# Cross-attention keys moved from after the first block into its woven steps

## Chip, core and metric

The kernel runs on one core of one Trainium2 chip. The metric is device time in microseconds (us) of one execution. All work is in fp32 precision, made of two fp32r parts (a high part and the remainder), so that a product of matrices is three matmuls: high by high, high by low, low by high.

## What is computed

Two transformer blocks run one after the other over 1024 tokens of width 1024. The first has a sliding-window attention and a gated convolution side by side, an output projection and a feed-forward layer. The second has three attentions side by side, then a cross attention to a memory of 256 rows, then a feed-forward layer. Only the cross attention's keys and values, which need the memory and no token, are touched by the change:

```python
def _cross(h, m, w_cq, w_ckv, w_co):
    q = (h @ w_cq).reshape(b, s, CROSS_HEADS, CROSS_DIM)
    k, v = jnp.split(m @ w_ckv, 2, axis=-1)
    ...
x = x + _cross(_rmsnorm(x, norm_cross[l]), _rmsnorm(mem, norm_mem[l]), ...)
```

## The kernel before, in words

Every activation is held transposed, in tiles of 128 features by 512 tokens (a half `h` of 0 or 1), each with a high and a low part. Weights stream from one packed tensor, 128x512 at a time (a slot of four 128x128 blocks): `Weights.block` (line 124) loads a slot on SP's queue, ScalarE (ACT) casts the high part, and the low part is made in one of two ways. While `W.adding` is set (line 778 to line 1583, the whole first attention and convolution), ACT writes the negated copy and a DMA issued by GpSimd (POOL) adds to it (line 143); afterwards VectorE (DVE) subtracts (line 145). There are 3 buffers for raw slots and 8 for each part, and loads keep their order.

The first block's work is woven by hand. `weave_all` (line 231) walks over main steps, which are matrix products yielding after each tile, and after each yield it runs as many side jobs from one ordered list as the step's rate has paid for. `SEQ` names the main steps: `k` keys and values, `a b c d` the queries of four head pairs, `G H` two convolution inputs, `o` the output projection over the first two of eight feature tiles (16 tiles of six matmuls: 8 output rows for half 0, then 8 for half 1), `P` the convolution's pointwise product and its part of the output projection for half 1. `SRATES` holds a rate for each. The side jobs are 17 attention steps (`swa`, piped by one), two convolutions (`convolve`, 47 vector multiply-adds each), `first_cat`, which fetches the first attention outputs back through DRAM, and the layer norm of the convolution for half 1 and half 0 (`normed`). Whether `"x"` is in `SEQ` decides where the memory is normed (`cross_norm`, line 1017) and where its keys are computed (`cross_keys`, line 1040): with it, the norm is a job of no cost at place `XNJ` of the list and the keys are a main step; without it, `cross_norm` is called behind the last woven product (after line 1109), and `cross_keys` behind the second half's output projection, just ahead of `cross_values`:

```python
    gemm(out1, 2, cat, ..., group=8, k0=2, x0=2, halves=(1, 0))
    if not mem_normed:
        mem_normed.append(cross_norm())
    x = load_x()
    ...
    add_post(x, mixed, rmix, "mix_post", 1)
    sums.first(x.cut(1))
    run(out1b(0, rmix))
    ...
    if "x" not in SEQ:
        run(cross_keys())
    if "X" not in SEQ:
        run(cross_values())
```

`load_x` (line 1121) reads the residual again; `add_post` (line 1123) adds the normed first half of the block to it; `sums.first` prepares the operands of the feed-forward layer, of whose products (`p`, seven for each tile) the first group is called `p5` and needs the sums `s1`.

Tiles with the tag `v` (128x512 fp32) are drawn from a common stock of `BUFS["v"]` buffers. The normed input `hn` takes 32 of them until the last queries (`d`) are done and the bias table `t5` takes 4; `cross_norm` asks for 4 tiles for the memory and 8 for its normed parts, and the normed parts live until keys and values are done. `cross_norm` takes its PSUM tile from the tag `mm` (7 buffers), which also holds every projection's output and the tiles `mu` and `bc` of the layer norms, and its scratch from `tmp` (3 buffers), which `add_post` uses next. Which instruction is issued when on each engine is fixed before the run by a list scheduler, from the program's order and the buffers, and isn't adapted to the chip.

Of the kernel before, what the change touches and what calls it, by code (L numbers as in the profile page):

```python
# [36 lines left out]
MERGE = 0  # L37
MLAPER = 1.8
FOXPER = 1.1
BUFS = {'phi': 6, 'plo': 6, 'hi': 2, 'lo': 3, 'fs': 2, 'v': 36, 'u': 8, 'p': 4, 'g': 4, 'mm': 7, 's': 3, 't': 3, 'o': 2, 'tmp': 3, 'evt': 3, 'stg': 2, 'rbc': 3, 'turn': 2, 'pt': 2, 'small': 20, 'csmall': 8, 'wraw': 3, 'whi': 8, 'wlo': 8, 'x': 58, 'y': 16, 'ge': 12, 'wt': 5, 'wq': 7, 'r': 16, 'sum': 4, 'rsum': 3, 'f': 6, 'l': 3}  # L40
NPRE = (4, 2)
TAIL = 2
BYPOOL = (0, 0)
# [24 lines left out]
STARTP = 200  # L68
XNJ = 8
GATES = (1, 2)  # L70
SEQ = "kabGHcdoP"
SRATES = (0.0, 0.0, 0.0, 0.75, 0.75, 1.0, 1.0, 2.0, 1.5)
SWACOST = 1.0
PLUS = ()
CONV2 = 3
# [20 lines left out]
class Weights:  # L96
# [27 lines left out]
    def block(self, mat, k, c0, w=P):  # L124
# [6 lines left out]
        if off == 0:  # L131
            s = pos // 4
            raw = self.pool.tile([P, 512], F32, tag="wraw", name=f"wraw{s}", bufs=BUFS["wraw"])
            self.load(raw, s)
            hi = self.pool.tile([P, 512], F32R, tag="whi", name=f"whi{s}", bufs=BUFS["whi"])
            lo = self.pool.tile([P, 512], F32R, tag="wlo", name=f"wlo{s}", bufs=BUFS["wlo"])
            if s in FIRSTW:
# [14 lines left out]
    def quarter(self, mat, k, c0, n=4, step=1):  # L152
# [3 lines left out]
        s = len(self.order) // 4  # L156
        raw = self.pool.tile([P, 512], F32, tag="wq", name=f"wraw{s}", bufs=BUFS["wq"])[:, :n * P]
        self.load(raw, s, n * P)
# [3 lines left out]
    def parted(self, raw, eng=None):  # L162
        self.made += 1
        w = raw.shape[-1]
        hi = self.pool.tile([P, 512], F32R, tag="phi", name=f"xhi{self.made}", bufs=BUFS["phi"])[:, :w]
        lo = self.pool.tile([P, 512], F32R, tag="plo", name=f"xlo{self.made}", bufs=BUFS["plo"])[:, :w]
        self.nc.scalar.copy(hi, raw)  # L167
# [63 lines left out]
def weave_all(mains, jobs):  # L231

    due = 0.0
    jobs = list(jobs)
    ended = 0
    for main, per, *need in mains:
        while need and need[0] in jobs:
            due -= jobs[0].cost  # L240
            jobs.pop(0)()
        for w in main:
            due += per * w
            while jobs and due >= jobs[0].cost and jobs[0].after <= ended:
                due -= jobs[0].cost
                jobs.pop(0)()
        ended += 1
    for j in jobs:
        assert j.after <= ended
        j()  # L250


def job(f, cost=1.0, after=0):
    f.cost, f.after = cost, after
    return f
# [26 lines left out]
def run(main):  # L282
    for _ in main:
        pass
# [3 lines left out]
def encoder_decoder_kernel(ctx: ExitStack, tc: tile.TileContext, a: dict, order_out: list):  # L288
# [728 lines left out]
    def cross_norm():  # L1017
        mem = [vt("mem") for _ in range(4)]
        ms = [mem[i // 2][:, (i % 2) * 256:(i % 2) * 256 + 256] for i in range(8)]
        with tc.issue_after(W.last.ins):  # L1020
            for i in range(8):
                nc.sync.dma_start(ms[i], a["memT"][tsl(i), :])
        both = {}

        class Mem:
            def hi(self, k, h):
                if k not in both:
                    both[k] = vt("memn", F32R)
                return both[k][:, 0:256]

            def lo(self, k, h):
                return both[k][:, 256:512]

        mn = Mem()
        norm_apply(ms, mn, 0, "norm_mem", rstd(sumsq(ms), D, psum=mmps))
        return mn
# [3 lines left out]
    def cross_keys():  # L1040
        mn = mem_normed[0]
        for i in range(4):
            if i % 2 == 0:
                xk_ = vt("xk")
            bl = [W.block("xk", k, i * P) for k in range(8)]
            ps = mmps("xk")
            mm3(ps[:, :256], [(bl[k], (mn.hi(k, 0), mn.lo(k, 0))) for k in range(8)])
            with tc.high_priority(offset=EVP):
                copy(xk_[:, (i % 2) * 256:(i % 2) * 256 + 256], ps[:, :256])
            if i % 2:  # L1050
                nc.sync.dma_start(zx[i // 2], xk_)
            yield 0.5

    def cross_values():
        def ev_xv(t, ps):
            u = vt("xv")
            copy(u, ps)
            nc.sync.dma_start(zx[2 + t], u)

        yield from vgemm_steps("xv", 8, mem_normed[0], 2, ev_xv)  # L1060
# [20 lines left out]
    def pos(key):  # L1081
        return SEQ.index(key) + 1

# [10 lines left out]
    norm_job = job(lambda: mem_normed.append(cross_norm()), 0.0)  # L1094
    if "x" in SEQ:
        jobs.insert(XNJ, norm_job)
# [3 lines left out]
    for i in range(4):  # L1100
        mains["abcd"[i]] = lambda i=i: queries(i)
    ln_job = [j for j in jobs if getattr(j, "half", None) == 1][0]
    early = int("P" in SEQ)
    needs = {"P": (ln_job,), "o": (cat_job,), "x": (norm_job,)}
    weave_all([(mains[key](), SRATES[n]) + needs.get(key, ())
               for n, key in enumerate(SEQ)], jobs)

# [477 lines left out]
    for pr, names in zip(pre, AHEADW):  # L1585
        for name in names:
            pr.get(name)
# [4 lines that stand above are left out]
# [675 lines left out]
```

## Time and profile before

| | us |
|---|---|
| median of three runs (2411.0 to 2414.62) | 2414.3 |
| the profiled execution, its own time | 2412.51 |
| its span in the trace | 2410.7 |
| TensorE (PE) busy | 2347.0 (97%) |
| VectorE (DVE) busy | 1752.9 (73%) |
| ScalarE (ACT) busy | 1139.9 (47%) |
| GpSimd (POOL) busy | 267.2 (11%) |

The busy times are of the one profiled execution. A matmul counts as busy until its modelled end, so two that overlap in the pipe are counted once; what a matmul costs is read from the distance between starts. In the rows, an arrow in square brackets gives the time for which an engine had been idle before an instruction, and what ended the wait.

### The profile page before, as it was taken

The numbers are of one execution on the slowest core, as the hardware profiler recorded it, in microseconds if no ns is written. First come the engines' busy times: TensorE is split into PE (matmuls) and PEld (weight loads), VectorE is DVE, ScalarE is ACT, GpSimd is POOL, SyncE is SP. The second block draws the span as 40 slices with busy tenths as digits, with TensorE's granted clock in tenths as the row PEclk, the third lists the DMA queues.
The fourth block names the chain that finished last, engine by engine and source line by source line (L and its number), as shares of the span: only waits on it lengthen the run. The fifth ranks groups of instructions, "written<-read, shape, count | busy, mean of one in ns | idle before, by whom it ended". The sixth has DMA issues, their size and how long they took to land.

```text
span 2410.7 us, 34720 instructions
## 1 busy us (share of the span) xinstructions
PE 2347.0 (97%) x11892; PEld 1894.6 (79%) x11892; DVE 1752.9 (73%) x3391; ACT 1139.9 (47%) x2313; POOL 267.2 (11%) x343
## 2 busy tenths in 40 slices
PE   9999799999999999999999999998999999999998
PEld 7877587687788887878887778887888888877886
DVE  7999659997777656688545576787797777666667
ACT  6355555545555543234444353545554555452222
POOL 2110121012111100000001110000011111110000
PEclk9999899999999999999999999999999999999999
DMA  7532278359867799724644465123237768699952
GB/s 206 121 82 58 49 155 296 115 146 280 228 173 215 200 373 366 253 78 152 186 119 147 142 201 181 40 58 101 79 103 199 208 173 219 178 276 379 353 173 77
DMA packets 235025, 430.09 MB, mean 178 GB/s; under 512 B 26112, under 2 KB 38752, under 8 KB 234848
## 3 DMA queue, kind: packets, MB, share of 16 engines
q1 hardware_dynamic: 197872, 350.71, 42.9%
q0 software_dynamic: 36688, 76.97, 16.1%
q8 instruction: 94, 1.54, 0.3%
q14 instruction: 83, 0.68, 0.1%
q10 hardware_dynamic: 288, 0.18, 0.0%
HBM read 246.10 MB, written 126.62 MB: 155 GB/s over the span
## 4 chain that ended last, share of the span: by engine, by line
PE 81%; DVE 9%; DMA 6%; issue 2%; ACT 1%; POOL 0%; SPq 0%; DVEq 0%; POOLq 0%; ACTq 0%
PE p L538 9%; PE p L540 9%; PE p L539 9%; PE mm L539 8%; PE mm L538 8%; PE mm L540 8%; PE low L540 5%; PE low L538 5%; PE low L539 5%; PE tp L589 2%; PE lo L1920 1%; DMA ff<-zff 1%; DMA wraw<-wstream 1%; PE fo L603 1%; DVE conv L839 1%
## 5 line engine op out<-in xcount | busy, mean ns | idle before, releaser
L538 PE MATMUL p<-s,xhi 128*128 128x512 f32 x704 | 276.6, 394 | 0.6 <-ACT xhi L167 0.5
L539 PE MATMUL p<-s,xhi 128*128 128x512 f32 x704 | 277.0, 393 | 0.0
L540 PE MATMUL p<-s,xlo 128*128 128x512 f32 x704 | 271.6, 394 | 1.3 <-DVE xlo L168 1.3
L538 PE MATMUL low<-ff,xhi 128*128 128x512 f32 (+1 forms) x628 | 246.7, 393 | 4.2 <-ACT xhi L167 4.2
L540 PE MATMUL low<-ff,xlo 128*128 128x512 f32 (+1 forms) x628 | 244.8, 393 | 2.8 <-DVE xlo L168 2.8
L539 PE MATMUL low<-ff,xhi 128*128 128x512 f32 (+1 forms) x628 | 246.5, 392 | 0.0
L167 ACT CAST xhi<-wt 128x512 fp32r<-128x512 f32 (+1 forms) x248 | 148.7, 607 | 180.7 <-DVE wt L178 90.2
L538 PE MATMUL p<-x,xhi 128*128 128x512 f32 x528 | 209.0, 396 | 3.3 <-ACT lo L1307 1.7
L540 PE MATMUL p<-x,xlo 128*128 128x512 f32 x528 | 206.4, 395 | 1.9 <-DVE xlo L168 1.9
L539 PE MATMUL p<-x,xhi 128*128 128x512 f32 x528 | 207.7, 393 | 0.0
L168 DVE TENSOR_TENSOR xlo<-wt,xhi 128x512 fp32r<-128x512 f32 (+1 forms) x248 | 166.1, 673 | 52.2 <-ACT xhi L167 38.6
L168 DVE TENSOR_TENSOR xlo<-wraw,xhi 128x512 fp32r<-128x512 f32 (+1 forms) x228 | 150.5, 665 | 45.2 <-DMA lo<-s 10.7
L167 ACT CAST xhi<-wraw 128x512 fp32r<-128x512 f32 (+1 forms) x228 | 134.0, 599 | 97.3 <-PE low L539 60.3
L540 PEld LDWEIGHTS p<-s,xlo 128*128 128x128 f32 x704 | 132.2, 188 | 32.7 <-DVE xlo L168 2.5
L538 PEld LDWEIGHTS p<-s,xhi 128*128 128x128 f32 x704 | 132.2, 188 | 32.7 <-ACT xhi L167 2.1
L539 PEld LDWEIGHTS p<-s,xhi 128*128 128x128 f32 x704 | 132.2, 188 | 30.6
L538 PEld LDWEIGHTS low<-ff,xhi 128*128 128x128 f32 x628 | 119.1, 190 | 32.2 <-ACT xhi L167 5.3
L540 PEld LDWEIGHTS low<-ff,xlo 128*128 128x128 f32 x628 | 119.1, 190 | 30.6 <-DVE xlo L168 3.9
L539 PEld LDWEIGHTS low<-ff,xhi 128*128 128x128 f32 x628 | 119.0, 190 | 26.8
L1308 POOL DMA_DIRECT2D lo<-u x82 | 71.5, 881 | 540.2 <-ACT lo L1307 358.3
L140 ACT CAST whi<-wraw 128x512 fp32r<-128x512 f32 x143 | 86.7, 616 | 87.5 <-DMA wraw<-wstream 56.4
L538 PEld LDWEIGHTS p<-x,xhi 128*128 128x128 f32 x528 | 99.1, 188 | 29.0 <-ACT xhi L167 3.0
(433 smaller groups left out, 5576.1 us busy)
## 6 DMA issues: line engine op xcount, KB each, us to landing
wraw<-wstream SPq DMA_DIRECT2D x408, 256.0 KB, 3.4
ff<-zff SPq DMA_DIRECT2D x308, 256.0 KB, 5.3
zff<-hi SPq DMA_DIRECT2D x154, 256.0 KB, 4.5
zff<-lo SPq DMA_DIRECT2D x154, 256.0 KB, 4.3
lo<-u POOLq DMA_DIRECT2D x82, 256.0 KB, 5.0
lo<-s POOLq DMA_DIRECT2D x66, 256.0 KB, 6.1
wlo<-wraw POOLq DMA_DIRECT2D x56, 256.0 KB, 3.9
res<-zres SPq DMA_DIRECT2D x48, 256.0 KB, 5.9
```

What stands on the lines that cost most here:

```text
L140: nc.scalar.copy(hi, raw)
L167: self.nc.scalar.copy(hi, raw)
L168: ins = (eng or self.nc.vector).tensor_tensor(lo, raw, hi.bitcast(F32), op=ALU.subtract)
L538: nc.tensor.matmul(ps, lhsT=ah, rhs=bh, start=first and i == 0, stop=False, skip_group_check=shared)
L539: nc.tensor.matmul(ps, lhsT=ah, rhs=bl, start=False, stop=False, skip_group_check=shared)
L540: nc.tensor.matmul(ps, lhsT=al, rhs=bh, start=False, stop=last and i == n - 1, skip_group_check=shared)
L589: nc.tensor.transpose(ps[:, tsl(j)], pr[:, c0 + (g + j) * P:][:, :P], ident)
L603: nc.tensor.matmul(o[j * 64:j * 64 + 64, :P], lhsT=value(g + t, j), rhs=pts[j][t], start=g + t == 0, stop=g + t == nt - 1)
L839: nc.vector.scalar_tensor_tensor(d, s_, col, d, ALU.mult, ALU.add)
L1308: nc.gpsimd.dma_start(lo, t, accum_op=ALU.add)
L1920: nc.tensor.matmul(o[:, tsl(j)], lhsT=lv[t][:, h * P:h * P + P], rhs=pt[t], start=t == 0, stop=t == i)
```

## The change

The letter `x` enters `SEQ` between `d` (the last queries) and `o` (the output projection), with a rate of 1.0, and the stock of `v` buffers grows from 36 to 38. By the two conditions quoted above, `cross_norm` becomes a side job that the planner reaches at the end of step `c`, `cross_keys` runs between `d` and `o`, and both calls later on fall away. `cross_values` stays. As the keys now run while `W.adding` is set, the low parts of their eight weight slots are made by ACT and a POOL DMA.

```diff
-BUFS = {..., 'v': 36, ...}
+BUFS = {..., 'v': 38, ...}
...
-SEQ = "kabGHcdoP"
-SRATES = (0.0, 0.0, 0.0, 0.75, 0.75, 1.0, 1.0, 2.0, 1.5)
+SEQ = "kabGHcdxoP"
+SRATES = (0.0, 0.0, 0.0, 0.75, 0.75, 1.0, 1.0, 1.0, 2.0, 1.5)
```

## Rows read from the trace of the kernel before

**Rows 1.** The page, busy time by engine: the tensor engine.

```profile
PE 2347.0 (97%) x11892; PEld 1894.6 (79%) x11892; DVE 1752.9 (73%) x3391; ACT 1139.9 (47%) x2313; POOL 267.2 (11%) x343
```

**Rows 2.** Busy time by stretch: stretch, its length, then each engine's busy time.

```profile
core 0: us, PE busy (x) PEld busy (x) DVE busy (x) ACT busy (x) POOL busy (x), PEclk, DMA share, GB/s
160.00:200.00 40.00, 40.00 (x234) 30.65 (x233) 37.15 (x96) 20.68 (x58) 5.51 (x8) 1.00 0.40 91
200.00:240.00 40.00, 37.37 (x268) 28.82 (x268) 40.00 (x128) 24.58 (x79) 2.77 (x4) 0.91 0.11 33
240.00:268.00 28.00, 14.53 (x99) 9.11 (x98) 23.24 (x53) 13.83 (x44) 3.03 (x5) 0.79 0.00 0
268.00:300.00 32.00, 29.86 (x141) 22.68 (x141) 17.00 (x32) 20.84 (x39) 8.20 (x9) 0.87 0.43 90
300.00:350.00 50.00, 50.00 (x239) 40.37 (x238) 29.55 (x51) 27.69 (x52) 11.67 (x14) 1.00 0.69 152
350.00:384.00 34.00, 34.00 (x156) 27.75 (x154) 24.31 (x48) 16.36 (x32) 8.04 (x10) 1.00 0.90 278
384.00:480.00 96.00, 86.33 (x440) 68.89 (x439) 94.53 (x157) 58.04 (x103) 6.87 (x5) 0.96 0.52 173
480.00:520.00 40.00, 39.87 (x179) 32.04 (x179) 39.89 (x67) 16.92 (x31) 1.48 (x2) 1.00 0.39 108
```

**Rows 3.** Timeline of PE, 260 to 270: start, length, line, tiles, idle before.

```profile
260.56 2.08 PE L995 MATMUL mu<-lns,constr 128*128 128x512 f32 x2 [5.99 <-DVE lns L987]
267.43 1.02 PE L498 MATMUL bc<-constr,sum 128*64 128x1 f32 x16 [4.79 <-DVE sum L455]
268.96 0.63 PE L539 MATMUL mm<-cat,whi 128*128 128x512 f32 x1
269.39 0.63 PE L540 MATMUL mm<-cat,wlo 128*128 128x512 f32 x1
```

**Rows 4.** Timeline of ACT and DVE: the output projection's tiles leave PSUM.

```profile
216.25 1.04 ACT L965 COPY mixed<-mm 128x512 f32<-128x512 f32 x2
...
271.34 0.69 DVE L963 COPY mixed<-mm 128x512 f32<-128x512 f32 x1 [2.69 <-PE mm L540]
```

**Rows 5.** DVE groups by shape, 300 to 380: the memory's norm (busy, mean ns).

```profile
L519 DVE SCALAR_TENSOR_TENSOR y<-mem,const,bc 128x256 f32<-128x256 f32 x8 | 3.6, 476 | 0.2 <-PE bc L507 0.2
L427 DVE TENSOR_TENSOR memn<-y,memn 128x256 fp32r<-128x256 f32 x8 | 3.3, 420 | 1.5 <-ACT memn L426 1.4
L452 DVE TENSOR_TENSOR sum<-sum,sq 128x256 f32<-128x256 f32 x6 | 2.3, 424 | 1.2 <-ACT sq L450 1.2
```

**Rows 6.** Tile view of `xk`: keys' matmuls and copies (ns min/median/max).

```profile
L540 PE MATMUL xk<-memn,wlo x32: 276/282/579, 384.2 to 407.5; 128*128 128x256 f32 x32
L422 DVE COPY xk<-xk x2: 411/414/416, 397.2 to 411.0; 128x256 f32<-128x256 f32 x2
```

**Rows 7.** Timelines of PE and DVE: distances between starts in the keys.

```profile
384.10 0.28 PE L539 MATMUL xk<-memn,whi 128*128 128x256 f32 x1
384.22 0.28 PE L540 MATMUL xk<-memn,wlo 128*128 128x256 f32 x1
...
386.70 1.28 DVE L145 TENSOR_TENSOR wlo<-wraw,whi 128x512 fp32r<-128x512 f32 x2
```

**Rows 8.** The page, DMA issues: the low parts made by accumulating DMAs.

```profile
wlo<-wraw POOLq DMA_DIRECT2D x56, 256.0 KB, 3.9
```

**Rows 9.** Timelines of PE, DVE, SP, 354 to 380: around the first residual add.

```profile
354.82 0.69 DVE L427 TENSOR_TENSOR cat<-mm,cat 128x512 fp32r<-128x512 f32 x1 [4.49 <-ACT cat L426]
...
357.07 0.60 PE L507 MATMUL bc<-const 128*128 128x128 f32 x4
...
365.60 11.92 SPq L703 DMA_DIRECT2D x<-xT  x13
...
366.15 0.47 DVE L519 SCALAR_TENSOR_TENSOR y<-mem,const,bc 128x256 f32<-128x256 f32 x1
367.48 0.74 DVE L1128 SCALAR_TENSOR_TENSOR pn<-mixed,const,bc 128x512 f32<-128x512 f32 x1
379.90 0.69 DVE L1130 TENSOR_TENSOR x<-x,pn 128x512 f32<-128x512 f32 x1 [1.43 <-DMA x<-xT]
```

**Rows 10.** Timelines of DVE and PE: the first feed-forward products.

```profile
402.90 0.40 PE L538 MATMUL p<-s,xhi 128*128 128x512 f32 x1
403.10 0.68 DVE L427 TENSOR_TENSOR s<-s,s 128x512 fp32r<-128x512 f32 x1
403.14 0.39 PE L539 MATMUL p<-s,xhi 128*128 128x512 f32 x1
```

More of the change, by code (lines that the diff above doesn't have):

```diff
@@ L39 @@
 FOXPER = 1.1
-BUFS = {'phi': 6, 'plo': 6, 'hi': 2, 'lo': 3, 'fs': 2, 'v': 36, 'u': 8, 'p': 4, 'g': 4, 'mm': 7, 's': 3, 't': 3, 'o': 2, 'tmp': 3, 'evt': 3, 'stg': 2, 'rbc': 3, 'turn': 2, 'pt': 2, 'small': 20, 'csmall': 8, 'wraw': 3, 'whi': 8, 'wlo': 8, 'x': 58, 'y': 16, 'ge': 12, 'wt': 5, 'wq': 7, 'r': 16, 'sum': 4, 'rsum': 3, 'f': 6, 'l': 3}
+BUFS = {'phi': 6, 'plo': 6, 'hi': 2, 'lo': 3, 'fs': 2, 'v': 38, 'u': 8, 'p': 4, 'g': 4, 'mm': 7, 's': 3, 't': 3, 'o': 2, 'tmp': 3, 'evt': 3, 'stg': 2, 'rbc': 3, 'turn': 2, 'pt': 2, 'small': 20, 'csmall': 8, 'wraw': 3, 'whi': 8, 'wlo': 8, 'x': 58, 'y': 16, 'ge': 12, 'wt': 5, 'wq': 7, 'r': 16, 'sum': 4, 'rsum': 3, 'f': 6, 'l': 3}
 NPRE = (4, 2)
```

## The prediction

> **What bounds the kernel now.** The page comes first: PE is busy 97% of the span [rows 1], so a change that leaves PE's work alone can gain only where PE waits. Busy time by stretch shows where that is near the keys [rows 2]. From 200 to 268 us PE is busy 51.9 of 68 us while DVE has no idle time up to 240: the first block's attention and convolutions keep DVE full, and PE waits for them. PE's timeline shows how that ends: 5.99 us of waiting for DVE's sums of the last convolution, then 4.79 us for the layer norm's squares [rows 3]. From 300 to 384 PE has no idle time and DVE has plenty. From 384 to 480, where the keys are now, PE lacks 9.7 us and DVE only 1.5: the residual add, the operand sums and the weight splits of the feed-forward layer are DVE's, and PE waits again. From 480 on PE is full. So there are two stages bounded by DVE with one bounded by PE between them, and the change moves work from the second to the first. What counts is what it moves on DVE.
>
> **The change, part by part.**
>
> *The keys on PE.* Four tiles of eight blocks and three matmuls are 96 matmuls of 256 columns. The tile view lists 32 for each of three lines [rows 6]; starts are 0.12 us apart where none waits [rows 7], so 11.5 us of PE work move. At the new place PE has 16.1 us without work (200 to 268, [rows 2]), so they fit and cost nothing there by themselves. If that cover is gone, the price is those 11.5 us.
>
> *The memory's norm on DVE.* It has 8 multiplies, 8 subtractions, 6 additions and a last addition: 3.6 + 3.3 + 2.3 us busy [rows 5] and 0.4 (one more addition at 424 ns), 9.6 us; with DVE's two copies of keys (0.41 us each, [rows 6]) 10.4. Back to back, DVE starts every 0.60 us an instruction that lasts 0.68 (two in 1.28, [rows 7]), so by that ratio 9.2 us. The job stands ahead of the last convolution in the list, so it goes ahead of the layer norm that PE waits for. It can use DVE's idle time ahead of 200, 2.9 us in 160 to 200 [rows 2], and I take half. The layer norm's sums come 9.2 - 1.5 = **7.7 us later** (bounds 0, if DVE's gaps took all of it, and 9.2).
>
> *Order on PE behind the layer norm.* Six of the output projection's sixteen tiles have left PSUM by 217; the seventh is multiplied only behind `bc` and leaves at 271.34 [rows 4]. That is where the list puts the layer norm: with rate 2.0 and two attention jobs ahead of it, it falls between the sixth and seventh tiles, and the later tiles, of the same tag `mm`, keep behind its `mu` and `bc`. With the change the two attention jobs are paid for by `x` (four yields of 0.5 at rate 1.0), so the layer norm falls behind the second tile. Four tiles that now run while PE would wait move behind it: 4 x 6 matmuls x 0.23 us between starts (402.90 to 403.14 is 0.24, [rows 10]) = **5.5 us later** (bounds 0, if the scheduler orders them otherwise, and 5.5).
>
> *The norm's few matmuls* leave the stage bounded by PE: a third of a `bc` group and two transposes (four take 0.60 us, [rows 9]), **-0.6**.
>
> *The low parts of the keys' weights.* DVE no longer makes them: 8 at a distance of 0.60 us [rows 7], 4.8, and with the two copies at 0.36 (0.41 by the same ratio) 5.5 us off the second stage. At the new place ACT makes 8 negated copies more and POOL issues 8 accumulating DMAs, each landing in 3.9 us [rows 8]. ACT is busy 38.4 of 68 us there and POOL 5.8 [rows 2]; I cost them at nothing. What is queued behind them: POOL's widening copies of the attention's reciprocals and SP's round trip of `first_cat`; PE waits for DVE longer than for either.
>
> *What the old place of the norm held up.* The norm of the mixed half is ready when its `bc` is transposed, at 357.07. But `add_post` starts at 367.48, behind the last scratch tile of the memory's norm (366.15), and the residual's loads start at 365.60, so that the first add waits for them until 379.90 [rows 9]. With the norm gone the scratch is free, and the loads need only `v` buffers, of which two are new. DVE idles 9.7 us between 350 and 384 [rows 2], and the norm's two passes there, 6.9 us busy [rows 5], about 6.1 at the ratio above, fall away: 15.8 us. Of these 4.49 [rows 9] and some 2 us of the norm lie ahead of the transposes and can't take the add. The other 9 can take most of `add_post` (16 instructions, 9.6 us at 0.60). So `s1`, whose last part now ends at 403.78 [rows 10], and what follows come 9 + 5.5 = **14.5 us earlier** against the stretch ahead. Bounds: 5.5, if the loads come no earlier; above, what PE leaves: its 9.7 us of waiting [rows 2] and the 11.5 us of the keys, 21.
>
> The sum against the profiled execution's own time of 2412.5 us (span 2410.7 and 1.8 around it; the median of the runs is 1.8 higher): 7.7 + 5.5 - 0.6 - 14.5 = -1.9. Against the median, 2414.3 - 1.9 = **2412.4 us**.
>
> *A rule weighed.* In 240 to 268 the granted clock is 0.79 on average, and right behind the waits matmuls start 0.43 us apart instead of 0.23 [rows 2, 3], which is the 1.2 GHz level after PE had idled. The Trainium skill ("TensorE: Matmul & The Clock Gate", Part 1) says that the throttled state is the default and activity releases it. By that rule the keys in these gaps would keep the clock up and give back up to ten such starts, 2 us, and the sum would be -4; by the rows alone PE still idles as long just ahead of `bc`, and the sum stays.
>
> **The rivals.**
>
> *The keys fill the gap, and the order gives* (faster). If the scheduler puts output tiles into PE's waits ahead of the layer norm, the 5.5 us don't arise, and tiles now behind `bc` (13.8 us of PE work in ten tiles) come ahead; what remains of the 7.7 is what the layer norm itself holds up, about 4. 4 - 0.6 - 14.5 = -11: 2403. For it: PE has 16 us there. Against it: the scheduler had that chance before and left 10.8 us of waiting next to tiles that were ready [rows 3, 4].
>
> *The residual's loads don't come earlier* (slower). SP's queue is in order, and the loads stand behind weight loads that wait for buffers. If the first is still issued some 20 us or less ahead of its first use's old time, the second stage gives back only the 5.5 us of DVE work and a little idle time, 7: 7.7 + 5.5 - 0.6 - 7 = +5.6, 2420. It decides from the point where the first load is issued less than 3 us earlier than now, measured from the end of the half's projection (350).
>
> *The keys don't get there* (slower still; the change doesn't do what it says). The memory and its normed parts need 12 `v` buffers, and 36 of 38 are taken until the last queries are done. If the normed memory comes so late that the keys fall behind the layer norm, their 11.5 us stand in the stage bounded by PE: 13.2 + 11.5 - 0.6 - 14.5 = +9.6, 2424. Against it: the queries end near 200, 60 us ahead of the layer norm.
>
> **How the numbers follow.** The forecast's case has 0.42, with a range of its own of 2405 to 2419 (halves of the two uncertain terms); the faster rival 0.28, the loads 0.22, the late keys 0.08. About 0.2%, 4.8 us, is what a measurement can tell from no change. Faster: 0.26 of the faster rival and 0.12 of the forecast's case. Slower: 0.13 of the loads, 0.07 of the late keys, 0.04 of the forecast's case. Same: the remaining 0.38. Eight times in ten the time should lie between 2399, which takes in the faster rival with a few us of clock, and 2422; both signs hold much of the chance.
>
> **What would show it.** Right, step by step: keys' matmuls between 200 and 250; `bc` of the first layer norm some 8 us later than 267.4, with two output tiles ahead of it and fourteen behind; the pointwise product some 13 us later; the first residual add directly behind the transposes of `bc`; `s1` some 14 us earlier against the end of the half's projection; PE full again from about 480. Wrong would be a `bc` no later than now (DVE had room), more than two output tiles ahead of it, or a first add still waiting for the residual's load. What would overturn the sum altogether is a later stage that moves: two more `v` buffers can change the order there too, and no row of before can price that.

## The result, and the profile after

| | before | after |
|---|---|---|
| median of four runs each, side by side (us) | 2413.0 (2411.0 to 2414.6) | 2425.4 (2424.0 to 2426.9) |
| profiled execution: span (us) | 2410.7 | 2425.1 |
| TensorE (PE) busy (us) | 2347.0 | 2356.2 |

The ratio is 1.0054, with a 95% interval of 1.0042 to 1.0066: the change makes the kernel slower by about 13 us. The forecast was 2412.4, with 2422 as its upper end.

The stretches of [rows 2] in the kernel after:

```profile
160.00:200.00 40.00, 37.87 (x222) 28.75 (x222) 37.99 (x108) 21.38 (x66) 3.97 (x6) 0.87 0.30 73
200.00:240.00 40.00, 37.10 (x237) 30.52 (x237) 38.14 (x103) 20.78 (x63) 6.27 (x9) 0.87 0.19 47
240.00:268.00 28.00, 22.38 (x132) 17.00 (x132) 20.24 (x47) 15.22 (x39) 7.42 (x10) 0.77 0.79 179
268.00:300.00 32.00, 28.38 (x160) 22.07 (x158) 20.34 (x54) 20.89 (x54) 2.70 (x3) 0.83 0.05 17
300.00:350.00 50.00, 45.37 (x212) 35.89 (x211) 23.27 (x40) 25.60 (x51) 11.38 (x14) 0.93 0.66 169
350.00:384.00 34.00, 31.16 (x141) 24.69 (x140) 16.12 (x26) 15.96 (x29) 9.14 (x11) 0.95 0.76 173
384.00:480.00 96.00, 90.83 (x400) 72.19 (x399) 84.24 (x136) 51.78 (x92) 7.18 (x9) 0.98 0.58 184
480.00:520.00 40.00, 32.82 (x141) 24.36 (x142) 36.52 (x62) 16.22 (x28) 7.24 (x2) 0.83 0.13 41
```

PE is busier between 240 and 268 (22.4 us against 14.5), as meant. But DVE, the engine that bounds this part, is *less* busy there (20.2 against 23.2), and PE now idles where it had no idle time at all: from 300 to 384, and from 480 to 520.

Where the time went is read best from a few instructions that both traces have, as the time from each to the next. "Last add" is the last addition that gathers the output projection of half 1, then of half 0; "gate" is the 577th `p` matmul with a low weight part in the first feed-forward layer; "cross" the first scores (`xs`) of the second block's cross attention; "gate 2" the 625th such `p` matmul, in the second block's feed-forward layer.

| us | start to layer norm's `bc` | to half 1's last add | to half 0's last add | to gate | to cross | to gate 2 | to the end |
|---|---|---|---|---|---|---|---|
| before | 267.4 | 81.9 | 42.2 | 444.2 | 796.4 | 117.2 | 661.2 |
| after | 284.8 | 93.6 | 38.4 | 444.5 | 793.6 | 110.5 | 659.7 |
| difference | +17.4 | +11.7 | -3.8 | +0.3 | -2.8 | -6.7 | -1.5 |

The differences make the +14.4 us of the spans. The first block loses 25.5 us up to the gate; 11 come back much later, in code that the change doesn't touch.

The rows that answer to [rows 3, 6, 9, 10], of the kernel after, from PE's timeline (start, length, line, tiles, idle before):

```profile
225.49 0.38 PE L538 MATMUL xk<-memn,whi 128*128 128x256 f32 x1
...
277.80 1.03 PE L995 MATMUL mu<-lns,constr 128*128 128x512 f32 x2
...
284.78 0.63 PE L498 MATMUL bc<-constr,sum 128*64 128x1 f32 x16 [3.62 <-DVE sum L455]
...
384.75 0.60 PE L507 MATMUL bc<-const 128*128 128x128 f32 x4
...
415.81 0.39 PE L538 MATMUL p<-s,xhi 128*128 128x512 f32 x1
```

and from SP's and DVE's:

```profile
333.30 2.58 SPq L703 DMA_DIRECT2D x<-xT  x5
```

```profile
385.39 2.06 DVE L1128 SCALAR_TENSOR_TENSOR pn<-mixed,const,bc 128x512 f32<-128x512 f32 x3 [1.78 <-PE bc L507]
387.98 1.89 DVE L1130 TENSOR_TENSOR x<-x,pn 128x512 f32<-128x512 f32 x3
```

The keys run from 225. The first of the residual's loads comes 45 us ahead of the end of half 1's projection (378.4), where it came 16 us behind it, and the first residual add stands 3.2 us behind the transposes of `bc` (387.98 - 384.75) where it stood 22.8 us behind them. All of that is as forecast. The layer norm's `bc` is 17.4 us later, where 7.7 were forecast.

### The profile page after: what moved, and what is told of

Its sections match the earlier page's. It is cut to its first block, busy times and chain, and to the rows that moved or that the text cites. A ratio compares the mean times of both kernels' runs of the same rounds, so it can differ in the third digit from the quotient of the medians.

```text
span 2425.1 us, 34725 instructions
## 1 busy us (share of the span) xinstructions
PE 2356.2 (97%) x11892; PEld 1903.3 (78%) x11892; DVE 1750.1 (72%) x3383; ACT 1142.6 (47%) x2321; POOL 282.8 (12%) x351
## 4 chain that ended last, share of the span: by engine, by line
PE 81%; DMA 7%; DVE 6%; issue 3%; ACT 2%; POOL 1%; SPq 0%; DVEq 0%; POOLq 0%; ACTq 0%
PE p L538 10%; PE p L540 10%; PE p L539 10%; PE mm L539 7%; PE mm L538 7%; PE mm L540 7%; PE low L538 5%; PE low L539 5%; PE low L540 5%; PE tp L589 2%; DMA wraw<-wstream 2%; PE lo L1920 1%; DMA x<-xT 1%; PE fo L603 1%; DMA zff<-lo 1%
## 5 line engine op out<-in xcount | busy, mean ns | idle before, releaser
L505 POOL TENSOR_TENSOR const<-const 128x4 f32<-128x4 f32 (+1 forms) x30 | 48.4, 1616 | 695.4 <-DVE const L502 695.4
```

The lines of the kernel that those rows point to most:

```text
L505: last_pow[0] = nc.gpsimd.tensor_tensor(r, v, neghalf[:, :nt], op=ALU.pow)
```

## The experiments

Fifteen kernels, each a change to the kernel after unless the text names another. Each ratio is to runs of the kernel before on the same chip, whose median was 2410.1 to 2410.8 us there. Places in time are from each kernel's one profiled execution. Where an edit moves or takes out the letter `x`, its rate in `SRATES` goes with it; that line is left out below.

### Why the layer norm comes 17 us later

**The memory's own buffers.** In the kernel after the last queries end at 223.1 and not at 194.1: half of the memory's loads wait for `v` buffers until 184.7, the norm's `bc` is multiplied at 209.1, and the last query tiles, of the same PSUM tag, stand behind it. The first suspicion was this knot.

```diff
-        mem = [vt("mem") for _ in range(4)]
+        mem = [slot("x", HALF)("mem") for _ in range(4)]
...
-                    both[k] = vt("memn", F32R)
+                    both[k] = slot("x", HALF)("memn", F32R)
```

> The changed kernel, but the memory and its normed parts draw on the buffers of the feed-forward operands, which are free at that time, and not on the 38 of tag v. In the changed kernel half of the memory's loads are issued only at 184.7 us, the norm's bc is at 209.1 and the last queries end at 223.1 instead of 194.1. Theory 'buffers' (the loads wait for buffers that the queries hold): all eight loads are issued near 99, bc comes before 190, the queries end before 205, the layer norm's bc falls from 284.8 to about 275 and the time from 2425.4 to 2413 to 2417. Theory 'tile order' (the norm's PSUM tile stands ahead of the last queries' tiles, and it is the norm's place on DVE that makes it late): the loads come early, but bc stays past 200 and the time within 3 us of 2425. Theory 'work' (only DVE's 9.6 us of norm and the order of output tiles count): the queries end earlier and the time stays within 3 us of 2425.

Measured: all eight loads at 98.5, the norm's `bc` at 180.9, the last queries done at 197.3. The knot is undone, and the layer norm's `bc` comes at 286.6, no earlier. 2430.6 us, ratio 1.0075 (1.0057 to 1.0093).

**The norm in another PSUM tag.**

```diff
-        norm_apply(ms, mn, 0, "norm_mem", rstd(sumsq(ms), D, psum=mmps))
+        norm_apply(ms, mn, 0, "norm_mem", rstd(sumsq(ms), D))
```

> The changed kernel, but the memory's norm takes its PSUM tile from the tag of the attention scores and not from that of the projections, so that the last queries' tiles don't stand behind it. Theory 'tile order': the queries end near 195 although the memory's loads are as late as in the changed kernel, the layer norm's bc falls from 284.8 to 275 to 278, and the time to 2415 to 2419. Theory 'buffers': with 36 of 38 taken the loads still come at 185 and the norm holds up the keys, so the time falls by no more than 5 us. Theory 'work': the queries end near 195 and the time stays within 3 us of 2425.

Measured: the queries end at 193.7 as before the change, yet `bc` comes at 287.1; 2438.4 us, ratio 1.0109 (1.0090 to 1.0127). DVE's longest waits here are for the attention's scores, 9.2 us, since the norm holds one of the three score tiles for a while: a side effect, so this run alone proves little. With the run above it rules out late queries as the cause.

**The norm early, the keys late.**

```diff
-SEQ = "kabGHcdxoP"
+SEQ = "kabGHcdoP"
...
-    if "x" in SEQ:
-        jobs.insert(XNJ, norm_job)
+    jobs.insert(XNJ, norm_job)
```

> The changed kernel with the memory's norm early and the keys left at their old place. Neither buffers nor tile order explained why the layer norm's bc comes at 284.8 and not at 267.4. Theory 'DVE work' (forecast's term: 7.7 us for the norm): bc at 274 to 276. Theory 'norm stalls the queue' (the norm's instructions wait in DVE's and ACT's fixed order for loads and for each other, and all of the 17 us is theirs): bc at 282 to 287. Theory 'keys' (their weights, copies and tiles hold up the last attention steps): bc at 267 to 271. For the time: the kernel with 38 buffers alone gave 2401.9; with the norm early the second stage should give back 9 us (scratch and loads) less what the first loses, so 2400 to 2402 by 'DVE work', 2408 to 2411 by 'norm stalls the queue', 2393 to 2396 by 'keys'.

Measured: `bc` at 271.6, a little under "DVE work" and just above "keys". The last queries are as late here (221.9) as in the kernel after, so once more they aren't the cause. 2418.3 us, ratio 1.0025 (1.0015 to 1.0035), slower than all three forecasts for the time; much of that gap arises behind half 0's last add, from which the gate is 449.8 us away here and 444.1 with 38 buffers alone. Busy time from 160 us to the layer norm's `bc` shows the shares. Columns as in [rows 2]: stretch, its length, busy PE, PEld, DVE, ACT, POOL, then clock and DMA. The kernel before, this one, and the kernel after:

```profile
160.00:267.40 107.40, 91.33 (x585) 67.99 (x584) 100.40 (x274) 59.09 (x181) 11.31 (x17) 0.92 0.19 46
```

```profile
160.00:271.60 111.60, 95.94 (x592) 73.27 (x590) 108.36 (x297) 63.53 (x193) 12.84 (x18) 0.86 0.19 48
```

```profile
160.00:284.80 124.80, 110.53 (x671) 85.98 (x670) 110.27 (x300) 69.75 (x207) 19.32 (x26) 0.84 0.35 83
```

The norm gives DVE 8.0 us more work, of which 3.8 go into its idle time (7.0 before, 3.2 here): +4.2 us. The keys give DVE only 1.9 us more work, but 11.3 us more *idle* time (14.5 after): +13.2 us.

**The keys with one weight slot; the keys with a quarter of their products.**

```diff
+        four = [W.block("xk", k, 0) for k in range(4)]
...
-            bl = [W.block("xk", k, i * P) for k in range(8)]
+            bl = four * 2
```

> The changed kernel with all 96 matmuls of the keys, but with one weight slot in place of eight (the same four blocks serve throughout, so the keys' values are not the reference's): ScalarE makes 14 weight instructions fewer there, and seven loads and seven accumulating DMAs fall away. With the norm early and the keys late the layer norm's bc was at 271.6, with both early at 284.8: the keys cost 13 us there. Theory 'weights' (ScalarE's casts wait for loads, and the attention's copies stand behind them): bc at 271 to 276 and 2413 to 2418 in time. Theory 'products' (the keys' matmuls, woven into the attention's last steps in a fixed order, lengthen its chain): bc at 281 to 287 and the time within 4 us of 2425.

```diff
-            mm3(ps[:, :256], [... for k in range(8)])
+            mm3(ps[:, :256], [... for k in (3, 7)])
```

> The changed kernel with all eight weight slots of the keys made, but with 24 of the 96 matmuls (only two of the eight blocks of each tile are multiplied, so the keys are not the reference's): 8.6 us of TensorE less. Theory 'weights': the layer norm's bc stays at 281 to 287 and the time within 4 us of 2425. Theory 'products': bc at 272 to 277 and 2414 to 2418.

Measured: `bc` at 275.8 with one slot and at 279.6 with few products. So 9.0 us go with the weights and 5.2 with the products; the two make 14.2, about the 13.2 us of both. Neither theory holds alone, the weights weigh more. The times are 2433.0, ratio 1.0091 (1.0076 to 1.0106), and 2421.7, ratio 1.0048 (1.0032 to 1.0064). The first has lost 8 of its 9 us again by the gate (860.3 against 861.3) and is 9 us slower from there to cross (802.4 against 793.6). TensorE's clock isn't what delays `bc`: from 160 us to `bc` its mean is 0.84 in the kernel after and 0.79 with few products, whose `bc` is the earlier one. How the weights can do it stands in the trace of the kernel after, in SP's timeline:

```profile
224.22 3.07 SPq L114 DMA_DIRECT2D wraw<-wstream  x2
227.67 0.33 SPq L938 DMA_DIRECT2D zc<-raw  x1
228.09 0.38 SPq L1011 DMA_DIRECT2D raw<-zc  x1
242.30 0.33 SPq L114 DMA_DIRECT2D wraw<-wstream  x1
242.72 0.41 SPq L1011 DMA_DIRECT2D raw<-zc  x1
243.91 3.12 SPq L114 DMA_DIRECT2D wraw<-wstream  x2
247.13 0.39 SPq L1011 DMA_DIRECT2D raw<-zc  x1
251.97 0.33 SPq L114 DMA_DIRECT2D wraw<-wstream  x1
252.35 0.44 SPq L1011 DMA_DIRECT2D raw<-zc  x1
```

and in ACT's and DVE's, with DVE's waits for that cast from 160 us to `bc` (in total, times, longest):

```profile
256.37 0.62 ACT L140 CAST whi<-wraw 128x512 fp32r<-128x512 f32 x1 [4.62 <-DMA wraw<-wstream]
```

```profile
259.80 0.69 DVE L427 TENSOR_TENSOR cat<-raw,cat 128x512 fp32r<-128x512 f32 x1 [3.54 <-ACT cat L426]
```

```profile
DVE cat L427 <- ACT cat L426: 5.1, 3, 3.5
```

The four loads that fetch the first attention outputs back (`raw`, line 1011) stand among the keys' weight loads in SP's queue and spread over 24 us, 228 to 252; with one weight slot they go out together, 228.2 to 231.2. ACT waits for a weight slot, the cast of `cat` behind it is late, and DVE waits for that cast with the last convolution's steps standing behind it. ACT's waits for weight slots from 224 to 286 are 7.7 us in all here, and they are gone with one slot, as are DVE's 5.1 us. That is the path in this trace, not the only one: in the kernel with the memory's own buffers and in the next one DVE waits for this cast only 1.6 and 1.5 us, and `bc` is about as late.

**The low parts by DVE.**

```diff
+            W.adding = False
             bl = [W.block("xk", k, i * P) for k in range(8)]
+            W.adding = True
```

> The changed kernel, but VectorE makes the low parts of the keys' eight weight slots, as it did at their old place: ScalarE's eight negated copies and POOL's eight accumulating DMAs fall away, VectorE has 8 subtractions (4.8 us) more. One weight slot instead of eight brought the layer norm's bc from 284.8 to 275.8, so the weights cost 9 us there. If that is the copies and the accumulating DMAs: bc at 278 to 282 in spite of VectorE's 4.8 us. If it is the loads, for which ScalarE waits with the attention's copies behind it: bc at 284 to 290, no better than the changed kernel, and the time 2424 to 2430.

Measured: `bc` at 283.6, at the edge of the second answer and outside the first: without the eight negated copies and accumulating DMAs, and with 4.8 us more on DVE, nearly the same. ACT still waits 6.1 us for the slots, and the `raw` loads still spread. This points to the loads and doesn't prove it: DVE's own 4.8 us may have cost up to as much, so of the 9.0 us up to 6.0 could still belong to the copies and accumulating DMAs. 2432.0 us, ratio 1.0099 (1.0079 to 1.0120).

### The order of the output tiles, and the keys' place

```diff
-SRATES = (0.0, 0.0, 0.0, 0.75, 0.75, 1.0, 1.0, 1.0, 2.0, 1.5)
+SRATES = (0.0, 0.0, 0.0, 0.75, 0.75, 1.0, 1.0, 0.0, 2.0, 1.5)
```

> The changed kernel with rate 0 for the keys' step instead of 1, so that six output tiles and not two come ahead of the convolution's layer norm, as before. Forecast's term: 5.5 us back, 2420. Theory 'order costs more': in the changed kernel the pointwise product starts 25.4 us behind the layer norm's transposes against 9.5 before, so up to 15 us come back: 2410 to 2413. Theory 'late queries' (what is late is late already ahead of the layer norm, and the output tiles only fill): within 3 us of 2425.

Measured: six tiles ahead of the layer norm again, its `bc` at 284.6 as in the kernel after, and then half 1's last add 13.0 us earlier (365.4 against 378.4). The advantage shrinks to 7.7 us at half 0's last add (409.1 against 416.8), 3.3 at the gate (858.0 against 861.3) and nothing in the time: 2427.5 us, ratio 1.0064 (1.0044 to 1.0084). The third answer, by its time; the second, by its first 100 us.

```diff
-SEQ = "kabGHcdxoP"
+SEQ = "kabGHcdoxP"
```

> The changed kernel with the keys' step behind the output projection's first part and not ahead of it, so that they fall behind the layer norm for which TensorE waits, into the stage where it is full. If the keys' 13 us at the layer norm come from standing between it and the attention: bc at 270 to 274 as with the norm alone early, the first half's projection ends at 362 to 367 instead of 378.4 (353.0 with the norm alone, and 11.5 us for the keys). If the second stage is bounded by half 0's operands and the keys were a free cover there, the time is 9 to 13 us above the kernel with the norm alone early, 2427 to 2431; if TensorE bounds it, the same as that, 2416 to 2420.

Measured: `bc` at 271.8, as with the norm alone, so the keys cost the layer norm nothing once they are behind it. Half 1's last add comes at 375.4, not at 362 to 367, and half 0's at 413.4 against 393.6 with the norm alone: in the stage where PE was full the 11.5 us cost 20, as PE now also waits there (11.2 us idle from `bc` to half 1's last add, against 2.6). 2429.2 us, ratio 1.0082 (1.0066 to 1.0098): the time is the one that the half-0 theory gave, but the loss lies ahead of half 0's last add, and that way wasn't foreseen.

### Why the second stage gives nothing back

**The keys a second time at their old place; half 0 first.**

```diff
-    if "x" not in SEQ:
-        run(cross_keys())
+    run(cross_keys())
```

> The changed kernel with the keys computed a second time at their old place: 96 matmuls (11.5 us of TensorE) and 5.5 us of VectorE more. If TensorE or s1 bounds the second stage, as the forecast has it: 11 to 17 us slower than the changed kernel, 2436 to 2442. If half 0's operands bound it (its bc comes at 437.2, 59 us behind the end of the first half's projection, against 51 before) and the keys only covered that wait: 2422 to 2429, no change or little.

```diff
-    run(out1b(0, rmix))
-    bc = rstd(rmix.total(0), D)
+    with tc.high_priority(offset=400):
+        run(out1b(0, rmix))
+        bc = rstd(rmix.total(0), D)
```

> The changed kernel with the second half's pointwise product, output projection and norm put ahead of the first half's sums in the scheduler's priority, nothing else. If half 0's chain bounds the second stage: its bc comes at 410 to 420 instead of 437.2 and the time falls by 8 to 15 us, 2410 to 2417, although the feed-forward products then begin later than 415.8. If the s1 chain bounds it, as the forecast has it: the products begin later and the time goes up by as much, 2428 to 2440.

Measured: with the keys twice, 11.5 us of PE work more, the gate is at 861.0 (861.3 in the kernel after). But half 1's last add is 6.4 us earlier there (372.0) and half 0's 3.8 (413.0), so the work isn't free: counted from these two places the gate is 6.1 and 3.5 us later. With half 0 first its `bc` comes at 422.0 instead of 437.2 and the products begin at 433.9 instead of 415.8, and the gate is at 862.6: one earlier, the other later, so this run shows only that neither sets the gate alone. The old tile order, above, has both about 12 us earlier than the kernel after (425.2 and 403.8), and the gate only 3.3. So PE's work counts for a third to a half of its length, and an earlier `bc` and earlier products for little. The times, 2434.7, ratio 1.0095 (1.0078 to 1.0112), and 2432.5, ratio 1.0085 (1.0068 to 1.0102), speak otherwise: the first is just under the answer for a bound by PE, the second within that for `s1`. But nearly all of the difference to the kernel after arises behind the gate, 4 and 7 us of it from gate to cross (797.7 and 800.4 us, the kernel after 793.6), where neither edit reaches.

**The residual add ahead of the norm, in the kernel before with 38 buffers.**

```diff
     sums.first(x.cut(1))
+    if not mem_normed:
+        mem_normed.append(cross_norm())
     run(out1b(0, rmix))
...
-    if not mem_normed:
-        mem_normed.append(cross_norm())
```

> The kernel before with 38 buffers, and the memory's norm not ahead of but behind the residual add and the first sums; keys and values stay. This takes the forecast's 9 us (scratch, residual's loads) alone. If s1 bounds the second stage: 9 us less than with 38 buffers alone, about 2393. If half 0's operands bound it: 2399 to 2404, no change.

Measured: 2424.2 us, ratio 1.0048 (1.0033 to 1.0062), worse than both answers, and not a clean test: the keys are now late with their norm (409.6 to 422.0), and half 0's projection with them (last add 63.4 us behind half 1's, instead of 42.1).

**Less work for DVE there**, in the kernel after (the values' weights) and in the kernel before with 38 buffers (keys' and values'): the line that ends `W.adding` goes behind `cross_values`.

```diff
-    W.adding = False
...
     if "X" not in SEQ:
         run(cross_values())
+    W.adding = False
```

> The changed kernel, with the low parts of the values' eight weight slots made by ScalarE and an accumulating DMA too, as those of the keys, so that VectorE loses 8 subtractions (4.8 us) between 400 and 435. Between the end of half 0's projection and the end of the gate's products lie 444.5 us in the changed kernel and 444.1 with 38 buffers alone, though the keys lie in the latter and not in the former. If VectorE bounds that stretch: the gate's products end 4 to 6 us earlier (last milestone 861.3) and the time is 2418 to 2422. If it is the order in which the engines take half 0's chain and the products: within 3 us of 2425.

> The kernel before with 38 buffers, and the low parts of the keys' and values' sixteen weight slots made by ScalarE and accumulating DMAs: 9.6 us of VectorE less between 384 and 435, with keys and norm at their old place. If VectorE bounds that stretch: 5 to 9 us faster than with 38 buffers alone (2401.9), 2393 to 2397, and that would be the keys' gain without their move. If the order bounds it, or ScalarE's waits for loads: 2400 to 2408.

Measured: the gate at 861.1 in the first, as in the kernel after, and 2435.3 us, ratio 1.0101 (1.0084 to 1.0118); the second 2432.1, ratio 1.0086 (1.0071 to 1.0101), 30 us slower than with 38 buffers alone. PE's waits in the second, 384 to 450 us (in total, times, longest):

```profile
PE xk L540 <- DMA wlo<-wraw: 10.0, 3, 4.7
PE vm L539 <- DMA wlo<-wraw: 8.1, 4, 2.3
```

Where the weights are needed at once, the accumulating DMA stands on the path itself. So neither run tells what DVE's load is worth: in the first, too, PE waits 3.8 us for these DMAs, and the second has a layer norm 5.1 us later than with 38 buffers alone (271.5 against 266.3). In the kernel after DVE is busy 36.5 of the 40 us from 480 to 520 in which PE lacks 7.2, so DVE remains a candidate.

### What the two buffers do

```diff
-BUFS = {..., 'v': 36, ...}
+BUFS = {..., 'v': 38, ...}
```

> The kernel before with 38 buffers of tag v instead of 36 and nothing else. If the buffers alone bring what the changed kernel gains in the second block's cross attention (TensorE waits 5.8 us for xp before, 1.5 after; the milestones there move 7 us closer): 2405 to 2408, with the first block as before. If that gain comes from the keys' early end: 2411 to 2415, no change.

> The kernel before with 37 buffers of tag v and nothing else. From the end of the first cross scores to the second block's gate the kernel takes 117.2 us with 36 buffers and 110.4 to 110.8 with 38 in all kernels but one. If one buffer is enough: 110 to 111 there and 2402 to 2406 in time. If it takes two: 117 and 2409 to 2413.

Measured: with 38 buffers and nothing else 2401.9 us, ratio 0.9964 (0.9953 to 0.9975), **faster than both kernels**; with 37, 2408.2, ratio 0.9989 (0.9978 to 0.9999), between its two answers. The first block is the same (gate at 834.0 and 834.8, before 835.8). From cross to gate 2 the kernels take 117.2 us with 36 buffers, 115.3 with 37, and 110.2 to 110.8 with 38 in all but one (114.1, the norm alone early). PE's waits in that stage, of the kernel before and then of that with 38 buffers:

```profile
PE xs L538 <- ACT xp L2041: 5.8, 2, 5.0
PE xo L2054 <- DVE xo L427: 0.4, 1, 0.4
```

```profile
PE xs L540 <- DVE xq L427: 1.6, 1, 1.6
PE mm L539 <- DVE xo L427: 0.9, 1, 0.9
```

In this stage PE runs 624 matmuls in both; with 38 buffers it idles 3.8 us less and is busy 3.0 us less with the same work, at a mean clock of 1.00 instead of 0.97. Why the wait for `xp` goes with the buffers stays open.

So the change consists of two: two buffers that bring 8.6 us at a place where the keys aren't touched, and the move of norm and keys, which costs about 22 (1.0054 against 0.9964). By the time of the kernel with the norm alone early (1.0025), about 15 of the 22 go with the norm and 7 with the keys; at the gate, in the profiled executions (834.0, 843.4, 861.3), it is 9.4 and 17.9. Behind the gate the kernel after is 6.4 us faster than the one with the norm alone (1563.8 against 1570.2); what makes that difference wasn't tested.

## Why the prediction was wrong, step by step

**The norm on DVE, 7.7 us: right in kind, too high.** 8.0 us of work (9.2 forecast), 3.8 of it in idle time (1.5 forecast), 4.2 us of delay; 5.3 against the kernel with 38 buffers alone, whose `bc` comes at 266.3.

**The keys at nothing: wrong, 13.2 us.** "They fit and cost nothing there by themselves" counted PE's 16.1 us without work as room. It wasn't room: PE still idles 14.3 us between 160 and `bc`, and `bc` is later. In this stage PE, ACT and DVE hand each step of the attention to one another in a fixed order, and DVE, which bounds it, idles 11.3 us more with the keys put between. The forecast named POOL's widening copies and SP's round trip of `first_cat` as what would be queued behind the keys' weights, and dismissed them because "PE waits for DVE longer than for either". That is the first step that failed: DVE itself waits for what stands behind them. With one weight slot in place of eight, 9.0 of the 13.2 us were gone.

**The order of the output tiles, 5.5 us: right in kind.** Two tiles came ahead of `bc` and fourteen behind, as forecast. The price was 13.0 us at half 1's last add, 7.7 at half 0's, 3.3 at the gate and nothing in the time. The surplus at half 1 has a visible cause, PE's waits from 268 to 384 us in the kernel after:

```profile
PE bc L498 <- DVE sum L455: 8.3, 2, 4.6
PE mm L538 <- DVE mixed L970: 2.8, 1, 2.8
```

3.6 of the first line are the layer norm of half 1 [rows 3 has 4.79 for it]; the other 4.6 are that of half 0, which in the kernel before lay under the pointwise product's matmuls and waited 0.5 us. The later pointwise product no longer covers it.

**The second stage, -14.5 us: the mechanism came, the gain didn't.** The loads came early, the first add followed the transposes, and the products began 37.4 us behind half 1's last add instead of 53.5, 16 us earlier and more than was forecast. But the gate is reached 444.5 us after half 0's last add, as before (444.2). The forecast followed one chain, `s1`, and took its end for the end of the stage: the second step that failed, 14.5 us forecast and 3.5 measured, all of it ahead of half 0's last add. PE's waits from 400 to 560 us show what was late next, before (5.9 us in all, the two longest lines) and after (13.0 us):

```profile
PE p L540 <- DVE xlo L168: 3.2, 3, 1.4
PE bc L507 <- POOL const L505: 2.4, 1, 2.4
```

```profile
PE bc L507 <- POOL const L505: 4.0, 1, 4.0
PE p L538 <- ACT xhi L167: 3.1, 4, 1.2
PE p L539 <- DVE x L1203: 3.0, 1, 3.0
PE p L539 <- DVE s L427: 1.6, 3, 0.7
PE p L538 <- ACT x L1202: 1.3, 1, 1.3
```

The early products run into operands that aren't there: `x`, `s`, weights. From half 0's last add to the gate, before and after:

```profile
391.60:835.80 444.20, 433.58 (x1920) 347.90 (x1921) 356.79 (x577) 245.95 (x449) 63.01 (x69) 0.99 0.69 196
```

```profile
416.80:861.30 444.50, 426.99 (x1845) 341.61 (x1844) 345.73 (x557) 234.17 (x429) 71.50 (x72) 0.98 0.66 188
```

PE has 75 matmuls fewer, 58 of them keys, and is busy 6.6 us less; all of that turns into idle time (10.6 us before, 17.5 after). Of 17 kernels, 15 take 442 to 450 us for this stretch, though their products begin anywhere from 400 to 434. Which operand sets that length stays open; DVE's load isn't excluded. That the waits of [rows 2] (9.7 us of PE in 384 to 480) would vanish was assumed, not worked out.

**PE full from 480: wrong.** It is busy 32.8 of 40 us from 480 to 520, against 39.9 [rows 2].

**The buffers at nothing: wrong, 8.6 us.** The last sentence of the forecast names this ("two more `v` buffers can change the order there too, and no row of before can price that"), but no chance and no width were given to it.

**PE's own time, taken as fixed: wrong.** The forecast started from "a change that leaves PE's work alone can gain only where PE waits", and its sum priced waits alone. From the start to the gate, before and after:

```profile
0.00:835.80 835.80, 801.97 (x3858) 639.01 (x3859) 671.96 (x1269) 453.66 (x912) 131.78 (x157) 0.98 0.61 165
```

```profile
0.00:861.30 861.30, 819.23 (x3858) 653.71 (x3859) 668.42 (x1261) 455.74 (x920) 145.13 (x165) 0.96 0.60 162
```

PE runs 3858 matmuls in both. Of the 25.5 us lost by the gate only 8.2 are more idle time; 17.3 are longer busy time for the same work, at a mean clock of 0.96 instead of 0.98. With the two levels of 1.2 and 2.4 GHz these means stand for about 69 us at the lower level against 33 (an estimate from the two means). So a wait costs more than its own length where PE then runs at the lower level, as from 480 to 520: the clock there was 1.00 without waits [rows 2] and is 0.83 with 7.2 us of them. This tells how the loss shows on PE, not what began it.

**The rule weighed.** The Trainium skill ("TensorE: Matmul & The Clock Gate", Part 1) says that activity releases the throttle. The forecast weighed that the keys in the gaps would by this rule keep the clock up. With them, the granted clock from 240 to 268 us is 0.77, and was 0.79 [rows 2]: PE is busier but still idles just ahead of `bc`, and nothing came back there.

**The rivals.** The late-keys rival gave 2424 and stood at 0.08; the time came out at 2425.4. Its first half happened: the buffers held the memory's loads until 184.7, and the queries ended at 223.1, which the forecast's objection ("the queries end near 200") had excluded. Its second half didn't: the keys ran from 225 to 246, ahead of the layer norm. And with the loads at 98.5 and the queries done at 197.3 the layer norm was as late. So the number was near for another reason. The residual's-loads rival fell by its own test (loads from 333.3); the faster rival by its own too (two output tiles ahead of `bc`, not more).

Laid side by side, 7.7 + 0 + 5.5 - 0.6 - 14.5 was forecast, and 4.2 + 13.2 + 11.7 - 3.5 came, and behind the gate -11.0 where nothing was forecast: +14.6 us by the rounded table, +14.4 by the spans. As the parts are distances between the same instructions, they must add up; that they do proves none of the causes.

## What to carry to other kernels

Idle time of an engine is room only where its neighbours don't wait for it step by step; before costing moved work at nothing, ask for each queue that its loads and casts pass through who stands behind them, and what the bounding engine takes from *those*. A chain that ends earlier is worth only the distance to the chain that ends next, so follow every operand of the next stage and not only the first one. Where the work is the same, compare the bounding engine's busy time too, and not its waits alone. And a change made of two edits deserves two prices: here one line of buffers was worth 8.6 us and hid 40% of what the other cost.

## What the runs showed of the hardware and hadn't been expected

- PE waits for none of the accumulating DMAs in the first block's attention of the kernel after. With sixteen slots made in that way where the matmuls follow at once, it waited 18.1 us for them.
- The same 3858 matmuls kept PE busy 802.0 us in one order and 819.2 in another, at a mean granted clock of 0.98 and 0.96.
- Stages that an edit doesn't touch still move: from gate to cross the 17 kernels took 793.6 to 802.5 us without any edit there. Each is a single profiled execution, and runs of the kernel before alone lay between 2406.8 and 2417.6 us on one chip, so how much of these 9 us belongs to the kernels isn't known. A gain of less than that has to be read at the stage that was edited, and not from the total alone.
